# Context stream beside the expert feed-forward: two column tiles of weights in one load, keys and values of two tiles projected in a row, four products of a projection at a step

## The chip, the cores and the metric

One core of one Trainium2 chip runs the whole program as a single launch. The metric is the device time of that launch in microseconds (us); before the change the median of three runs is 2534.96 us (2532.47 to 2540.46). Engines are named as in the profile: PE is TensorE (PEld its weight loads), DVE VectorE, ACT ScalarE, POOL GpSimd, SP SyncE. SP does no arithmetic here; it issues nearly all DMA loads, one after the other.

## What is computed

The reference runs two blocks one after the other. The first mixes tokens and then applies an expert-choice feed-forward with 16 experts; the second works on the output of the first (the "latent" tokens, `x` below) and on a separate context sequence of 256 tokens. Cut to what matters:

```python
def reference(x, ...):
    x = first_block(x, ...)             # token mixer, then 16 experts of 1024 -> 2816 -> 1024
    return second_block(x, ctx_2, ...)  # context and latents through w_in_2, then 32 small experts

def _expert_choice_ffn(h, ...):
    xs = u[idx]                         # 34 rows for each expert
    hid = silu(xs @ w_gate) * (xs @ w_up)
    y = (hid @ w_down) * g              # scattered back by idx

def mixing_sublayer(u_lat, u_ctx, ...):
    a_ctx, b_ctx, _ = split(u_ctx @ w_in)       # independent of the first block
    _, state_a = run_a(a_ctx, zeros_a)          # gated delta rule, 4 heads, two directions
    _, state_b = run_b(b_ctx, zeros_b)          # RWKV, 8 heads, two directions
    oa_lat, _ = run_a(a_lat, state_a)           # the latents start from the context's states
    ob_lat, _ = run_b(b_lat, state_b)
```

The context's part (projections of `u_ctx` and the two final states) does not depend on the first block, so the kernel can do it at any time before the latents are mixed.

## The kernel before

The program has three stages. `head` does the first block's token mixer. `ffn` does the 16 experts. `lat` does the second block: the latents' mixing, the merge and the second expert layer.

**The experts.** `expert` (L881 to L927) takes an expert in three chunks of hidden columns (1024, 1024 and 768 of 2816). For a chunk it loads `w_gate` and `w_up` (four loads each, of 1024 KB or 768 KB) and `w_down` (four loads, or three in the last chunk, of 1024 KB). The rows of an expert fill only 64 columns of the PE array, so products come in pairs: two products, of 64 columns each, run side by side (the loop over `h` at L890 for the tile `gu`, over `dc` at L908 for the tile `dn`). An expert has 70 such pairs and 35 loads. In the profile an f32 product counts as two instructions, so a pair is four. Between `gu` and `dn` stand the activation (`hid`, L896 to L898) and its transposes (`hb` L902, `hT`). The loads of all experts go through a ring of ten buffers of 1 MB; SP waits at each load for PE to be done with the buffer's last content.

**The context stream.** `ctx_pre` (L930) is a Python generator that issues the context's work in small steps. From expert 1 on, `paced` (L869) counts pairs, and after a pair it lets the stream take as many steps as are due: `CTX_STEPS * pairs // CTX_PAIRS`, with 470 steps spread over 1000 of the 1050 pairs (L62). The stream's instructions are issued after that pair (`beside`, L207). So on PE the stream's products stand between pairs of the experts. A scheduler then orders each engine's queue, and may move an instruction that isn't ready in its own reckoning a few places.

**The projections.** The stream has 18 projections of 128 columns of `w_in_2`: eight for the delta rule (`gdn_in` L1243: keys and values, two head pairs, two tiles each) and ten for RWKV (`mixed` L1418: two of low rank, then key and value for each of four column tiles `j`). `projc` (L1076) is one projection: eight products with the transposed context `cuT` (128x256 each, the full array of 128 columns) into one bank `pc`; it yields after each product, so a projection is eight steps. `rwkv_prep` (L1493) projects key and value of its own tile `j` and then goes on with the scaling and the recurrences of that tile.

**Its loads.** `ahead_loader` (L256) has four buffers of 512 KB and keeps three loads ahead of the projection that reads; a load is 128 columns, so a row of it in memory is 512 bytes. These loads stand on SP in between the experts' loads (the DMA issue itself is L252, in `loader`).

Of the kernel before, what the change touches and what calls it, by code (L numbers as in the profile page):

```python
# [10 lines left out]
F32 = mybir.dt.float32  # L11
# [5 lines left out]
P = 128  # L17
D = 1024
KD = D // P
# [39 lines left out]
LBANKS = dict(pa=2, pc=2, pd=1, pb=2, pe=1)  # L59
LPARTS = (3, 5)  # L60

CTX_STEPS, CTX_PAIRS = 470, 1000  # L62

PCOL, PCOL_N = _layout([
    ("mix_norm_g", 8), ("conv_w", 40), ("conv_b", 8), ("ret_gn_g", 4), ("mlstm_gn_g", 4),
# [97 lines left out]
class Net:  # L163
# [89 lines left out]
            return lambda k, cs=slice(None): t[:, k, cs]  # L253
        return load

    def ahead_loader(self, bufs, cols):  # L256

        get, todo, there = self.loader(bufs), iter(cols), []
        ahead = len(bufs) - 1

        def load(c):
            while len(there) < ahead + 1:
                n = next(todo, None)
                if n is None:
                    break
                there.append((n, get(n)))
            n, w = there.pop(0)
            assert n == c
            return w
        return load  # L270

    def rload(self, src):
# [657 lines left out]
    def ctx_pre(self):  # L930

        tc, nc, I = self.tc, self.nc, self.I
        self.SA = [self.S.tile([P, 4, P], F32, name=f"SA{d}") for d in range(2)]
        self.SB = [self.S.tile([P, 4, 64], F32, name=f"SB{d}") for d in range(2)]
        for s in self.SA + self.SB:
            nc.gpsimd.memset(s, 0.0)
        with tc.tile_pool(name="CW", bufs=2, reuse_waits="tile") as CW, tc.tile_pool(name="C", bufs=1, reuse_waits="tile") as C:
            bufs = [CW.tile([P, SLOTW], F32, name="w") for _ in range(2)]
            cols = [gi * 512 + hp * 256 + j * P for hp in range(2) for gi in (1, 2) for j in range(2)]
            cols += [2064 + ci * P for ci in [12, 13] + [4 * gi + j for j in range(4) for gi in (1, 2)]]  # L940
            load = self.ahead_loader([b[:, i * D:(i + 1) * D] for b in bufs for i in range(2)], cols)
            with tc.tile_pool(name="C0", bufs=1, reuse_waits="tile") as T:

                rw = T.tile([P, KD, 36], F32, name="crw")
                self.router_load(rw)
                src = T.tile([P, 2, D], F32, name="csrc")
                nc.gpsimd.dma_start(src, I["ctx_2"][0].rearrange("(t p) d -> p t d", p=P))
                yield
                b = self.bank("ebs")[:, :36]
                for k in range(KD):  # L950
                    nc.tensor.matmul(b, self.mcol[:, 0, 24 + k:25 + k].to_broadcast([P, P]), rw[:, k, :], start=(k == 0), stop=(k == KD - 1))
                    yield
                ob, _ = PROW["router_grp_b_2"]
                self.lbias = self.pers.tile([P, 36], F32, name="lbias")
                nc.vector.tensor_add(self.lbias, b, self.prow[:, ob:ob + 36])
                xn = T.tile([P, 2, D], F32, name="cxn")
                self.norm256(T, src, xn, "css")
                gs, sh = self.mod_cols(T, "norm_mix_g_2", 1, 0, 1, "cmc")
                yield
                uT = yield from self.affT(C, xn, gs, sh, "cuT")  # L960
            with tc.tile_pool(name="CG", bufs=1, reuse_waits="tile") as G:
                gates = yield from self.gdn_gates(G, uT)
                for hp in range(2):
                    qkv = []
                    yield from self.gdn_in(G, uT, False, hp, load, qkv)
                    x = yield from self.gdn_products(G, qkv, False)
                    for d in range(2):
                        yield from self.gdn_dir(G, d, False, 2 * hp, gates, x, self.SA, False, None)
            with tc.tile_pool(name="CR", bufs=1, reuse_waits="tile") as R:
                yield from self.rwkv(R, R, uT, self.SB, False, load, ("pb", "pb", "pb"))  # L970
# [102 lines left out]
            yield  # L1073
        return uT

    def projc(self, w, uT):  # L1076

        b = self.bank("pc")[:, :256]
        for k in range(KD):
            self.nc.tensor.matmul(b, w(k), uT[:, k, :], start=(k == 0), stop=(k == KD - 1))  # L1080
            yield
        return b

    def advance(self, queue, n):
# [158 lines left out]
    def gdn_in(self, W, uT, lat, hp, load, qkv):  # L1243
# [5 lines left out]
        for gi in range(0 if lat else 1, 3):  # L1249
            dst = W.tile([P, 2, 256], F32, name=f"gx{gi}", tag="giB" if gi == 2 and not lat else f"gx{gi}",  # L1250
                         bufs=2 if lat and gi < 2 else 1)
            for j in range(2):
                pj = yield from self.projc(load(gi * 512 + hp * 256 + j * P), uT)
                raw = W.tile([P, 256], F32, name="graw", bufs=1)
                nc.scalar.copy(raw, pj)
                c = 4 * gi + h0 + j
                cw = lambda k: self.pc("gdn_conv_2", c * 5 + k)
                tmp = W.tile([P, 256], F32, name="gcv", bufs=2)
                nc.vector.tensor_scalar(tmp, raw, cw(2), None, op0=ALU.mult)
                for k in (0, 1, 3, 4):  # L1260
                    s = k - 2
                    a, e = max(0, -s), 256 - max(0, s)
                    nc.vector.scalar_tensor_tensor(tmp[:, a:e], raw[:, a + s:e + s], cw(k), tmp[:, a:e],
                                                   op0=ALU.mult, op1=ALU.add)
                self.sigmoid(dst[:, j, :], tmp)
                nc.gpsimd.tensor_mul(dst[:, j, :], dst[:, j, :], tmp)
            if gi < 2:
                for j in range(2):
                    sq = W.tile([P, 256], F32, name="gsq", tag="gcv", bufs=2)
                    nc.scalar.activation(sq, dst[:, j], AF.Square)  # L1270
                    b = self.bank("gn")[:, :256]
                    nc.tensor.matmul(b, self.ct("ones"), sq, start=True, stop=True)
                    nc.scalar.activation(sq, b, AF.Ln, bias=self.eps)
                    nc.scalar.activation(sq, sq, AF.Exp, scale=-0.5)
                    nc.vector.scalar_tensor_tensor(dst[:, j], dst[:, j], 1.0 if gi else P ** -0.5, sq, op0=ALU.mult,
                                                   op1=ALU.mult)
                    if not lat:
                        yield
            qkv.append(dst)
# [112 lines left out]
    def rwkv(self, W, F, uT, S, lat, load, tags, start=None):  # L1392
# [24 lines left out]

        def mixed(ci, dst):  # L1418

            pj = yield from self.projc(load(B0 + ci * P), uT)  # L1420
            pad = F.tile([P, 258], F32, name="rpd", bufs=1)
            nc.gpsimd.memset(pad[:, 0:1], 0.0)
            nc.gpsimd.memset(pad[:, 257:258], 0.0)
# [28 lines left out]
        env = dict(W=W, F=F, lat=lat, na=na, T1=T1, Ne=Ne, lo=lo, nwa=nwa, omk=omk, mixed=mixed, S=S, tags=tags)  # L1452

        if not lat:
            for j in range(4):
                x = {}
                yield from self.rwkv_prep(j, env, x)
                for d in range(2):
                    yield from self.rwkv_scale(j, d, x, env)
# [35 lines left out]
    def rwkv_prep(self, j, env, x):  # L1495
# [7 lines left out]
            x["g2"] = W.tile([P, P], F32, name="rg2", bufs=2)  # L1503
            self.dma.dma_start(x["g2"], self.I["rwkv_g2_2"][0][:, j * P:(j + 1) * P])
        for gi, name in ((1, "k"), (2, "v"), (0, "r")):
            if lat or gi:
                x[name] = F.tile([P, 256], F32, name="rx" + name, bufs=1)
                yield from env["mixed"](4 * gi + j, x[name])
        kk = x["kk"] = F.tile([P, 256], F32, name="rkk")
# [744 lines left out]
```

## Time and profile before

| | us |
|---|---|
| median of three runs | 2534.96 |
| lowest and highest | 2532.47, 2540.46 |
| the profiled execution's own time | 2544.69 |
| its span, from the first to the last instruction | 2542.9 |
| experts' stage in it (first `gu` to last `dn`) | 294.9 to 1722.7, 1427.8 long |
| PE busy over the span | 2343.9 (92%) |

The profiled execution is 0.4% above the median of the runs. In the page the DMA engines are at nine tenths or more from a tenth of the span to two thirds of it, while PE is at nine tenths too, so the page alone doesn't tell which of the two sets the pace there; the rows below are read for that. A "busy" PE is only an engine with a matmul in its pipeline.

### The profile page before, as it was taken

Reading aid. Unit: us, or ns where it says so; the run is one execution under the profiler, and the core shown is the slowest. Engines: PE = TensorE matmul, PEld = TensorE weight load, DVE = VectorE, ACT = ScalarE, POOL = GpSimd, SP = SyncE. Lnnn points to the kernel's source line nnn. Section 1 sums busy time; section 2 is a strip of 40 time slices with the busy share of each in tenths; the row PEclk is TensorE's granted clock in tenths of the full one; section 3 lists DMA queues with packets and bytes.
Section 4 is the critical chain, followed back from the end, with each engine's and each line's share of the span. In section 5 each row is a group of like instructions: output and inputs, shape, how many; then the busy total and the mean of one; then the engine's idle time right before and its main releaser. Section 6 shows DMA issues by size and latency. Waiting matters only on the chain. (4 is left out here: it accounts for less than half of the span.)

```text
span 2542.9 us, 45236 instructions
## 1 busy us (share of the span) xinstructions
PE 2343.9 (92%) x18736; PEld 1251.7 (49%) x18736; DVE 994.2 (39%) x2419; ACT 655.4 (26%) x1652; POOL 350.8 (14%) x627
## 2 busy tenths in 40 slices
PE   7997799999989999999999999987988999989997
PEld 6765334334334333333334333336767777865564
DVE  6655311232222213313313313215576473645545
ACT  4443111221111112212112212214444333522221
POOL 3101100010000101101101101103253232300000
PEclk9998899999999999999999999998979788999999
DMA  7664999998999999999999999994301112689995
GB/s 242 228 235 140 332 407 403 400 400 331 401 382 337 394 369 379 396 397 383 374 409 377 389 407 390 377 407 119 93 22 45 44 27 60 227 273 363 367 366 186
DMA packets 328177, 755.07 MB, mean 297 GB/s; under 512 B 13088, under 2 KB 167376, under 8 KB 324896
## 3 DMA queue, kind: packets, MB, share of 16 engines
q1 hardware_dynamic: 326464, 747.67, 79.6%
q0 software_dynamic: 1504, 4.46, 0.6%
q8 instruction: 150, 2.46, 0.4%
q14 instruction: 59, 0.48, 0.1%
HBM read 751.03 MB, written 1.05 MB: 296 GB/s over the span
## 5 line engine op out<-in xcount | busy, mean ns | idle before, releaser
L891 PE MATMUL gu<-w,xs 128*64 128x512 f32 (+1 forms) x3072 | 682.1, 571 | 2.8 <-DMA w<-in_w_up 1.8
L909 PE MATMUL dn<-w,hT 128*64 128x512 f32 x1408 | 336.5, 604 | 19.1 <-ACT hT L317 17.4
L891 PEld LDWEIGHTS gu<-w,xs 128*64 128x64 f32 x3072 | 196.1, 137 | 289.2 <-issue 271.1
L1080 PE MATMUL pc<-luT,w 128*128 128x256 f32 x688 | 180.0, 403 | 0.5 <-ACT early L300 0.3
L909 PEld LDWEIGHTS dn<-w,hT 128*64 128x64 f32 x1408 | 88.7, 137 | 164.9 <-issue 132.1
L1080 PEld LDWEIGHTS pc<-luT,w 128*128 128x128 f32 x688 | 127.9, 197 | 18.6 <-ACT early L300 0.7
L2110 PE MATMUL egu<-w,exs 128*64 128x256 f32 x1024 | 123.2, 383 | 0.0
L897 DVE TENSOR_TENSOR hid<-hid,gu 128x512 f32<-128x512 f32 (+1 forms) x48 | 30.7, 640 | 203.4 <-ACT hid L302 197.4
L1080 PE MATMUL pc<-cuT,w 128*128 128x256 f32 x288 | 99.2, 429 | 0.0
L1080 PEld LDWEIGHTS pc<-cuT,w 128*128 128x128 f32 x288 | 43.3, 188 | 107.8 <-issue 104.3
L2110 PEld LDWEIGHTS egu<-w,exs 128*64 128x64 f32 x1024 | 74.6, 137 | 39.4 <-issue 6.9
L300 ACT ACTIVATE hid<-gu 128x512 f32<-128x512 f32 (+1 forms) x48 | 26.8, 559 | 238.1 <-PE gu L891 238.1
L1643 POOL TENSOR_SCALAR rsw<-rSU,rwc 64x64 f32<-64x64 f32 x112 | 38.2, 341 | 290.8 <-DVE rSU L1659 280.2
L898 DVE TENSOR_TENSOR hid<-hid,gu 128x512 f32<-128x512 f32 (+1 forms) x48 | 30.8, 642 | 113.4 <-PE gu L891 111.8
L1599 PE MATMUL rmt<-rT,rBK 128*128 128x128 f32 (+1 forms) x256 | 55.4, 361 | 20.3 <-DVE rT L1586 13.9
L2137 PE MATMUL edn<-w,ehT 128*64 128x512 f32 x256 | 67.7, 597 | 0.7 <-ACT ehT L317 0.5
L295 PE MATMUL pj<-uTh,wp 128*128 128x272 f32 x320 | 65.3, 298 | 0.0
L285 ACT CAST wp<-w 128x1024 fp32r<-128x1024 f32 (+1 forms) x48 | 55.0, 1186 | 39.4 <-DMA w<-in_w_in 20.5
L286 DVE TENSOR_TENSOR wp<-w,wp 128x1024 fp32r<-128x1024 f32 (+1 forms) x44 | 57.5, 1328 | 13.3 <-ACT wp L285 13.3
L1599 PEld LDWEIGHTS rmt<-rT,rBK 128*128 128x128 f32 x256 | 43.8, 225 | 35.6 <-POOL rBK L1564 16.2
L2153 DVE TENSOR_TENSOR acc<-acc,esc 128x512 f32<-128x512 f32 x64 | 41.0, 682 | 42.5 <-PE esc L2152 42.5
L295 PEld LDWEIGHTS pj<-uTh,wp 128*128 128x128 f32 x320 | 51.9, 193 | 8.2 <-issue 4.8
(675 smaller groups left out, 3512.1 us busy)
## 6 DMA issues: line engine op xcount, KB each, us to landing
w<-in_w_down SPq DMA_DIRECT2D x176, 1024.0 KB, 11.0
w<-in_w_gate SPq DMA_DIRECT2D x128, 1024.0 KB, 10.8
w<-in_w_up SPq DMA_DIRECT2D x128, 1024.0 KB, 12.3
w<-in_w_gate SPq DMA_DIRECT2D x64, 768.0 KB, 10.7
w<-in_w_up SPq DMA_DIRECT2D x64, 768.0 KB, 7.3
w<-in_w_in SPq DMA_DIRECT2D x65, 512.0 KB, 4.6
w<-in_moe_w_gate SPq DMA_DIRECT2D x32, 1024.0 KB, 13.2
w<-in_moe_w_up SPq DMA_DIRECT2D x32, 1024.0 KB, 12.2
```

Of the source, the lines that this page charges most:

```text
L285: self.nc.scalar.copy(hi, src)
L286: (eng or self.nc.vector).tensor_sub(lo, src, hi)
L295: self.nc.tensor.matmul(out, a[x], b[y], start=(i == 0 and x + y == 0), stop=(i == n - 1 and x == 1))
L891: ins = nc.tensor.matmul(b[h * 64:(h + 1) * 64, :w], xs[:, k, :], ws(k, slice(h * w, (h + 1) * w)), start=(k == 0), stop=(k == KD - 1))
L898: nc.vector.tensor_mul(hid, hid, gu[1][:, :w])
L909: ins = nc.tensor.matmul(dn[dc * 64:(dc + 1) * 64], hT[:, j, h * 64:(h + 1) * 64], wd(h * nf + j, slice(dc * 512, (dc + 1) * 512)), start= ...
L1080: self.nc.tensor.matmul(b, w(k), uT[:, k, :], start=(k == 0), stop=(k == KD - 1))
L1599: ins = nc.tensor.matmul(b[:, i], BK[:, c0 + i, h:h + 2, :], T[:, h, c0 + i, :, :], start=True, stop=True)
L1643: nc.gpsimd.tensor_scalar(sw[r], SU[r, h, c, :], wc[r, c:c + 1], 0.0, op0=ALU.mult, op1=ALU.add)
L2110: nc.tensor.matmul(b[64 * i:64 * i + 64, x * 256:x * 256 + 256], xs[:, k, i, :], w[i](k), start=(k == 0), stop=(k == KD - 1))
L2137: nc.tensor.matmul(b[64 * i:64 * i + 64, :], hT[:, j, 64 * i:64 * i + 64], wd[i](j, cs), start=(j == 0), stop=(j == 1))
L2153: nc.vector.tensor_add(h[:, t, cs], h[:, t, cs], b)
```

## The change

A projection yields after every fourth product where it belongs to the context (`every=4`), so it is two steps and not eight; the latents keep one product a step. `CTX_STEPS` falls from 470 to 362, which is the 18 times six steps fewer; they are still spread over 1000 pairs. Loads bring 256 columns, two neighbouring tiles, in one DMA of 1024 KB with rows of 1024 bytes, into two buffers; the first pair is loaded when the stream starts, and every first use of a pair starts the load of the next (`pair_loader`). In the RWKV part the keys of two tiles and the values of two tiles are projected in a row before the first of them goes on (`rxk` and `rxv` have two buffers each); `rwkv_prep` does no projection for the context any more.

```diff
-CTX_STEPS, CTX_PAIRS = 470, 1000
+CTX_STEPS, CTX_PAIRS = 362, 1000
...
-    def ahead_loader(self, bufs, cols):
-
-        get, todo, there = self.loader(bufs), iter(cols), []
-        ahead = len(bufs) - 1
+    def pair_loader(self, pool, cols):
+
+        todo, there = iter(cols), {}
+        src = self.I["w_in_2"][0]
+
+        def begin():
+            c = next(todo, None)
+            if c is not None:
+                t = pool.tile([P, KD, 2 * P], F32, name="w")
+                self.dma.dma_start(t, src[:, c:c + 2 * P].rearrange("(k p) c -> p k c", p=P))
+                there[c], there[c + P] = t[:, :, 0:P], t[:, :, P:2 * P]
 
         def load(c):
...
+            if c in cols:
+                begin()
+            t = there.pop(c)
+            return lambda k, cs=slice(None): t[:, k, cs]
+        begin()
         return load
...
-            cols = [gi * 512 + hp * 256 + j * P for hp in range(2) for gi in (1, 2) for j in range(2)]
-            cols += [2064 + ci * P for ci in [12, 13] + [4 * gi + j for j in range(4) for gi in (1, 2)]]
-            load = self.ahead_loader([b[:, i * D:(i + 1) * D] for b in bufs for i in range(2)], cols)
+            cols = [gi * 512 + hp * 256 for hp in range(2) for gi in (1, 2)]
+            cols += [2064 + ci * P for ci in (12, 4, 8, 6, 10)]
+            load = self.pair_loader(CW, cols)
...
-    def projc(self, w, uT):
+    def projc(self, w, uT, every=1):
 
         b = self.bank("pc")[:, :256]
         for k in range(KD):
             self.nc.tensor.matmul(b, w(k), uT[:, k, :], start=(k == 0), stop=(k == KD - 1))
-            yield
+            if k % every == every - 1:
+                yield
         return b
...
-                pj = yield from self.projc(load(gi * 512 + hp * 256 + j * P), uT)
+                pj = yield from self.projc(load(gi * 512 + hp * 256 + j * P), uT, 1 if lat else 4)
...
         if not lat:
+            xs = [{} for _ in range(4)]
             for j in range(4):
-                x = {}
+                x = xs[j]
+                if j % 2 == 0:
+                    for gi, name in ((1, "k"), (2, "v")):
+                        for i in range(2):
+                            xs[j + i][name] = F.tile([P, 256], F32, name="rx" + name, bufs=2)
+                            yield from mixed(4 * gi + j + i, xs[j + i][name])
                 yield from self.rwkv_prep(j, env, x)
...
-            if lat or gi:
+            if lat:
                 x[name] = F.tile([P, 256], F32, name="rx" + name, bufs=1)
```

On PE, where RWKV's first projections stand between the experts' pairs (`gu`, `dn`), before:

```order
L1080 MATMUL pc<-cuT,w 128x256
L891 MATMUL gu<-w,xs 64x512 x4
L1080 MATMUL pc<-cuT,w 128x256
L891 MATMUL gu<-w,xs 64x512 x4
L1080 MATMUL pc<-cuT,w 128x256
L891 MATMUL gu<-w,xs 64x512 x4
L1080 MATMUL pc<-cuT,w 128x256
L891 MATMUL gu<-w,xs 64x512 x6
L1080 MATMUL pc<-cuT,w 128x256
```

And the same place of the changed kernel (L895 is L891 there, L1083 is L1080):

```order
L895 MATMUL gu<-w,xs 64x512 x4
L1083 MATMUL pc<-cuT,w 128x256 x4
L895 MATMUL gu<-w,xs 64x512 x6
L1083 MATMUL pc<-cuT,w 128x256 x4
L895 MATMUL gu<-w,xs 64x512 x6
L1083 MATMUL pc<-cuT,w 128x256 x4
L895 MATMUL gu<-w,xs 64x512 x4
L1083 MATMUL pc<-cuT,w 128x256 x4
L895 MATMUL gu<-w,xs 64x512 x6
```

Products of a projection now stand four in a row, with two or three pairs of the experts in between. Over the whole stage the context's 144 products stand in 139 places before (138 alone, six once in a row) and in 30 places after (25 of four, four of eight, one of twelve).

On SP, the queue of loads at the same place of the program, the experts' loads with the stream's (`in_w_in`) among them, before:

```order
L241 DMA w<-in_w_up 128x2x768
L252 DMA w<-in_w_in 128x8x128
L241 DMA w<-in_w_up 128x2x768 x3
L279 DMA w<-in_w_down 128x2x1024 x3
L241 DMA w<-in_w_gate 128x2x1024 x2
L252 DMA w<-in_w_in 128x8x128
L241 DMA w<-in_w_gate 128x2x1024 x2
L241 DMA w<-in_w_up 128x2x1024 x4
```

And after, where the three last loads of the stream stand (L265 issues a pair):

```order
L241 DMA w<-in_w_gate 128x2x1024 x3
L265 DMA w<-in_w_in 128x8x256
L241 DMA w<-in_w_gate 128x2x1024
L241 DMA w<-in_w_up 128x2x1024 x4
L265 DMA w<-in_w_in 128x8x256
L283 DMA w<-in_w_down 128x2x1024 x4
L241 DMA w<-in_w_gate 128x2x768 x2
L265 DMA w<-in_w_in 128x8x256
```

Half as many loads of twice the size stand in the queue, five to eight of the experts' loads apart here; before, 14 loads of one tile stand among the experts' loads after expert 0, after, seven of two tiles (the rest is loaded ahead, at 14 loads into expert 0, in both).

## Rows read from the trace of the kernel before

**Rows 1.** The page: DMA engines' busy tenths and rate, 40 slices

```profile
DMA  7664999998999999999999999994301112689995
GB/s 242 228 235 140 332 407 403 400 400 331 401 382 337 394 369 379 396 397 383 374 409 377 389 407 390 377 407 119 93 22 45 44 27 60 227 273 363 367 366 186
```

**Rows 2.** Windows by expert (1, 2, 7, 11, 12, 14, 15): engines' busy us, clock, DMA

```profile
core 0: us, PE busy (x) PEld busy (x) DVE busy (x) ACT busy (x) POOL busy (x), PEclk, DMA share, GB/s
...
362.30:449.40 87.10, 83.51 (x411) 33.51 (x409) 16.80 (x39) 14.21 (x36) 0.93 (x1) 0.98 1.03 404
449.40:543.80 94.40, 89.69 (x468) 31.32 (x470) 25.85 (x56) 20.84 (x46) 6.34 (x8) 1.00 1.04 397
...
928.10:1019.40 91.30, 85.03 (x679) 32.81 (x679) 25.23 (x59) 18.82 (x45) 10.59 (x23) 1.00 1.01 386
...
1290.70:1380.90 90.20, 86.33 (x653) 31.89 (x651) 23.61 (x55) 17.30 (x40) 9.80 (x21) 1.00 1.00 387
1380.90:1468.00 87.10, 81.03 (x699) 33.61 (x697) 27.20 (x69) 17.41 (x45) 12.60 (x28) 1.00 1.01 394
...
1560.60:1650.20 89.60, 84.67 (x841) 34.37 (x841) 26.90 (x67) 17.56 (x45) 11.99 (x25) 0.98 1.00 378
1650.20:1722.70 72.50, 64.59 (x339) 22.09 (x339) 10.96 (x24) 8.42 (x18) 2.95 (x10) 1.00 1.03 399
```

**Rows 3.** The same view, the whole stage of the experts in one window

```profile
294.90:1722.70 1427.80, 1338.10 (x9522) 516.81 (x9522) 360.70 (x854) 252.16 (x593) 131.72 (x268) 0.99 1.00 386
```

**Rows 4.** Waits of the queue of loads (SP), 440 to 1700: us, times, longest

```profile
engine line waited for: us in total, times, longest us
SPq L241 <- PE gu L891: 396.2, 208, 8.4
SPq L241 <- PE dn L909: 205.7, 58, 9.0
...
SPq L252 <- PE pc L1080: 9.0, 14, 1.8
```

**Rows 5.** Waits of PE, 440 to 1700: us in total, times, longest

```profile
PE hb L902 <- DVE hid L898: 20.4, 31, 1.8
PE dn L909 <- ACT hT L317: 14.9, 25, 0.8
PE rmt L1599 <- DVE rT L1586: 13.9, 6, 3.1
```

**Rows 6.** Timeline of PE, a projection between pairs: start us, us, instructions

```profile
903.42 1.51 PE L891 MATMUL gu<-w,xs 128*64 128x384 f32 x8
904.86 0.70 PE L1080 MATMUL pc<-cuT,w 128*128 128x256 f32 x2
905.49 2.16 PE L891 MATMUL gu<-w,xs 128*64 128x384 f32 x12
907.58 0.70 PE L1080 MATMUL pc<-cuT,w 128*128 128x256 f32 x2
```

**Rows 7.** Timeline of PE in the latents' stage, eight products in a row

```profile
1913.00 3.72 PE L1080 MATMUL pc<-luT,w 128*128 128x256 f32 x16
```

**Rows 8.** Timeline of PE, steps of a recurrence between pairs

```profile
1402.12 1.94 PE L909 MATMUL dn<-w,hT 128*64 128x512 f32 x8 [0.69 <-ACT hT L317]
1403.98 0.33 PE L1647 MATMUL rp<-rP,rY 64*64 64x64 f32 x4
1404.25 1.94 PE L909 MATMUL dn<-w,hT 128*64 128x512 f32 x8
...
1414.80 4.51 PE L891 MATMUL gu<-w,xs 128*64 128x512 f32 x20
```

**Rows 9.** Windows of 25 us; in the second a load of the stream lands

```profile
600.00:625.00 25.00, 24.79 (x326) 9.94 (x324) 5.70 (x16) 2.73 (x7) 0.91 (x2) 0.92 0.68 230
...
925.00:950.00 25.00, 24.50 (x102) 7.64 (x98) 5.24 (x9) 3.83 (x7) 0.74 (x3) 1.00 1.04 400
1250.00:1275.00 25.00, 24.21 (x250) 10.37 (x250) 5.93 (x14) 1.91 (x5) 0.46 (x1) 1.00 0.88 322
...
1450.00:1475.00 25.00, 23.61 (x209) 10.34 (x209) 8.38 (x18) 4.81 (x13) 1.26 (x4) 1.00 1.03 410
```

**Rows 10.** The page's DMA issues: count, KB each, median us to landing

```profile
w<-in_w_gate SPq DMA_DIRECT2D x128, 1024.0 KB, 10.8
w<-in_w_up SPq DMA_DIRECT2D x128, 1024.0 KB, 12.3
```

**Rows 11.** Waits of the queue of loads over the whole span

```profile
SPq L252 <- PE pc L1080: 175.2, 39, 20.9
```

**Rows 12.** Waits of PE in the latents' stage, 1900 to 2230

```profile
PE rp L1632 <- DVE rSU L1659: 6.3, 4, 3.0
```

More of the change, by code (lines that the diff above doesn't have):

```diff
@@ L254, in loader @@
         return load
-    def ahead_loader(self, bufs, cols):
-        get, todo, there = self.loader(bufs), iter(cols), []
-        ahead = len(bufs) - 1
-        def load(c):
[L262 to L269, printed above, removed]
+    def pair_loader(self, pool, cols):
[7 more added lines that the diff above has]
+                there[c], there[c + P] = t[:, :, 0:P], t[:, :, P:2 * P]
+        def load(c):
+            if c in cols:
[3 more added lines that the diff above has]
+        begin()
         return load
@@ L937, in ctx_pre @@
         with tc.tile_pool(name="CW", bufs=2, reuse_waits="tile") as CW, tc.tile_pool(name="C", bufs=1, reuse_waits="tile") as C:
-            bufs = [CW.tile([P, SLOTW], F32, name="w") for _ in range(2)]
-            cols = [gi * 512 + hp * 256 + j * P for hp in range(2) for gi in (1, 2) for j in range(2)]
-            cols += [2064 + ci * P for ci in [12, 13] + [4 * gi + j for j in range(4) for gi in (1, 2)]]
-            load = self.ahead_loader([b[:, i * D:(i + 1) * D] for b in bufs for i in range(2)], cols)
+            cols = [gi * 512 + hp * 256 for hp in range(2) for gi in (1, 2)]
+            cols += [2064 + ci * P for ci in (12, 4, 8, 6, 10)]
+            load = self.pair_loader(CW, cols)
             with tc.tile_pool(name="C0", bufs=1, reuse_waits="tile") as T:
@@ L1418, in mixed @@
         def mixed(ci, dst):
-            pj = yield from self.projc(load(B0 + ci * P), uT)
+            pj = yield from self.projc(load(B0 + ci * P), uT, 1 if lat else 4)
             pad = F.tile([P, 258], F32, name="rpd", bufs=1)
```

## The prediction

> **What bounds the kernel now.** Everything the change touches lies in the experts' stage, so I read that stage alone, in this order. First the page's slices [rows 1]: from the sixth to the twenty-seventh the DMA engines are nine tenths busy or more nearly everywhere, at 331 to 409 GB/s. That looks like a stage set by its loads. Then the same stretch by expert [rows 2]: the DMA share stays near 1.0, but the rate moves between 378 and 404 GB/s, so the stream of weights is not always at its top. The top is seen in a window of 25 us without the context's loads [rows 9]: 410 GB/s at a share of 1.03; and 404 over the whole of expert 1 [rows 2]. In between it falls to 322 and even 230 GB/s [rows 9], while PE is busy 24 of 25 us.
>
> Who waits for whom settles it. SP, which issues the loads, waits 396.2 us in 208 waits for `gu` and 205.7 us in 58 for `dn` [rows 4]: the buffers are full, and a load goes out when PE has used one up. In PE's own waits [rows 5] the large ones are the experts' activation (20.4 and 14.9 us) and the stream's recurrences (13.9 us); no load is among them. So PE sets the pace here, with the DMA close behind. How close: the stage moves 386 GB/s x 1427.8 us = 551 MB [rows 3]. At expert 1's 404 GB/s that is 1364 us, 64 us less than the stage takes; at 410 it would be 84 less. PE's time can shrink by some 60 us before the loads bind the stage as a whole, less where they bind a part of it.
>
> **The change, part by part.**
>
> *Four products at a step.* No product is added or removed; what changes is how often the context's products cut into the experts' pairs. The price of one cut is read off the timeline [rows 6]. Eight instructions of `gu` last from 903.42 to 904.86, 1.44 us from start to start; twelve last from 905.49 to 907.58, 2.09 us. Four cost 0.65, so eight would cost 1.30 in an unbroken row, and the cut adds 0.14. The projection's one product (two instructions) holds PE from 904.86 to 905.49, 0.63 us. In a row such instructions come every (3.72 - 0.70)/14 = 0.216 us [rows 6, 7], 0.43 for two; so 0.20 more are the cut's. Together 0.34. With pairs of 512 columns [rows 8]: eight instructions take 1403.98 - 1402.12 = 1.86, in a row 8 x (4.51 - 1.94)/12 = 1.71, so 0.15 there: 0.35 a cut. The order of instructions shows 139 such places before and 30 after, 109 fewer: 109 x 0.35 = **38 us** of PE's time, nothing of it beside other work, since PE is what the stage waits for.
>
> *Fewer steps, spread over the same pairs.* An expert's 70 pairs take 32.9 steps before (470/1000) and 25.3 after. A step that is not a projection adds its matmuls and the cut, about 0.27 + 0.14 = 0.41 us for a small one [rows 8]. So the work moves: between projections an expert becomes lighter, by 7.6 steps or some 3 us; while projections run, heavier, as two steps now bring eight products. By the end of expert 6 the changed order has done 14 of 18 projections, the old one 11. The gain therefore comes late, from expert 7 on.
>
> *What the faster PE runs into.* An expert's weights are 27 loads of 1024 KB and 8 of 768, 34.6 MB, 85.6 us at 404 GB/s. Expert 1 takes 87.1 us at that rate already [rows 2]: its 7.6 fewer steps save next to nothing; I take back 4 us. Experts 11, 12 and 14 take 90.2, 87.1 and 89.6 us and would come down to 83 to 87, at or below 85.6. There the buffers that were full are drawn on; loads are issued ten buffers ahead, some 26 us, and land in 10.8 to 12.3 [rows 10], so some 14 us of work lies ready. Expert 15 has no steps after its first 20 pairs; it takes 72.5 us [rows 2], less than its loads' 85.6, because it lives on that reserve. What the others draw, expert 15 pays. Bounds: 0 (reserve as before) to 13 us (none left); I take 4, nearer to 0, since each run of projections fills it again.
>
> *Waits for the stream's own results.* With more pairs between steps, PE finds results ready more often: two thirds or so of the 13.9 us of `rmt` can go (-9). With a quarter fewer steps to fill the experts' activation gap, its 35.3 us [rows 5] can grow, by a sixth at most (+6), as few steps stood there. I take 0, between the two.
>
> *Loads of a pair.* Seven loads of 1024 KB for 14 of 512 among the experts' loads. The first reader of a pair comes after the last of the one before. One load after the other of the experts costs 2.6 us of the stream; a pair's costs that at least, and no more than two single ones. With a single one in it, a window of 25 us moved 400 GB/s at a share of 1.04, without it 410 [rows 9]: 10 x 25 = 0.25 MB, 0.6 us a load, up to 8 us of DMA for the 14, of which between nothing and all goes. DMA is not what sets the end, so I count 0. SP waits 9.0 us in 14 waits for the old loads' buffers, 1.8 at most [rows 4]; the new ones stand just as far ahead of PE, at the place where their buffer comes free.
>
> The Trainium skill, "DMA: Bandwidth & Descriptors", Specifications, gives 512 bytes as the least transfer for line rate, by which rows of 512 bytes already run at full rate and pairing them brings nothing at all. The trace is slightly against it (400 against 410 GB/s above), and by the rule the sum stays the same, since that term is 0 in it.
>
> *Keys and values of two tiles in a row.* This shifts eight projections and their work on ACT, POOL and DVE; each has two steps, some five pairs, between it and the next. I count 0. *The latents' stage* keeps its instructions, but the scheduler swaps some neighbours in its second half; PE's largest group of waits there is 6.3 us [rows 12]: 0, within 6 either way.
>
> Sum: -38 + 4 + 4 = **-30 us**. The profiled execution (2544.7, span 2542.9) would become 2515; the median of the runs, 0.4% lower, 2535 - 30 = **2505 us**.
>
> **The rivals.**
>
> *The stream of weights takes over.* For it: a share of 1.0 throughout and expert 1 at its top rate. Then experts 7 to 14, 722.1 us now (928.1 to 1650.2) [rows 2], can come down to 8 x 85.6 = 685 and no further (-37); expert 15 starts without a reserve (+13); and the three projections that move into the experts up to 6 bring 3 x 8 x 0.43 = 10 us of products there (+10), which the later ones give back only within that floor. -14, **2521**. Against it: the many full-buffer waits of SP and 64 us of room over the stage.
>
> The Trainium skill, same page and section, puts the limit of HBM for one core at about 358 GB/s, which would make the stream the bound all through. By that limit 551 MB would need 1539 us and nothing could be gained: 2535. The trace excludes it: the stage takes 1427.8 us and reaches 410 GB/s.
>
> *Waits shrink as well.* Wider spacing removes most of `rmt`'s 13.9 us, and the reserve holds in experts 1 and 15 (the two times 4 are not paid): -38 - 9 = -47, **2488**. For it: the longest of those waits, 3.1 us, is about what another pair between two steps gives. Against it: the activation's gap is then less often filled.
>
> *A pair's load holds up the queue: slower.* A pair waits on SP for the last reader of the buffer, and the experts' loads behind it wait too. In the experts' stage such waits reach 1.8 us; elsewhere in this kernel the same wait reached 20.9 [rows 11]. PE feels it once it is longer than the 14 us that lie ready. At 20.9 each of seven would cost 7 us: +49 - 30 = +19, **2554**. It decides from a wait of 14 + 30/7 = 18 us. Against it: the new loads stand in SP's queue some ten loads ahead of PE, as the old ones do.
>
> That the cuts would not become fewer is excluded by the order (30 places).
>
> **How the numbers follow.** The forecast (2495 to 2517) has 0.60, the stream of weights 0.20 (2512 to 2531), shrinking waits 0.10, the held queue 0.04; 0.06 is for shifts in the latents' stage and the activation's gap that eat the gain. A measurement of this kernel tells about 0.3% from no change, that is 7.6 us: faster means below 2527.4, slower above 2542.6. Faster: 0.60 + 0.10 + three quarters of 0.20 = 0.85; same: the other 0.05 and 0.05 of the last case, 0.10; slower 0.05. The range reaches from the shrinking waits to the upper end of the second case: 2487 to 2531, with 0.05 left out below and 0.12 above.
>
> **What would show it.** In the profile after, four products of a projection (eight instructions) should take about 1.9 us and the context's `pc` some 70 us busy (25 x 2.0 + 4 x 3.72 + 5.4, by [rows 7] and 0.216 an instruction) instead of 139 x 0.70 = 97; the stage from first `gu` to last `dn` about 1398 us, with the gain in experts 7 to 14 (83 to 87 us each, 402 GB/s or more) and expert 15 a few us longer. Waits of SP for `gu` and `dn` should fall. If PE's waits for loads appear in experts 7 to 15, the stream has taken over; if `rmt` waits vanish, the third case is there; waits of several us at the pairs' loads on SP with PE waiting for weights would be the fourth. The forecast is wrong at its root if `gu` takes longer in a row than 0.16 us an instruction at 384 columns once the cuts are gone.

## The result: 29 us less, most of it where it was expected

The changed kernel takes 2508.86 us (median of four runs, 2506.38 to 2513.87), the kernel before, beside it on the same chip, 2537.71 (2532.47 to 2546.12): a ratio of 0.9896, 95% interval 0.9875 to 0.9917, or 29 us. A second comparison, on another chip, gives 2512.48 against 2534.69, 0.9908 (0.9879 to 0.9937), 22 us. Forecast were 2505 and 30 us less. The sum came out; the runs below show that several of its terms did not, in opposite directions.

The page of the changed kernel, its DMA rows in 40 slices (they answer to [rows 1]) and the group of the context's projections (busy us, mean ns, idle before):

```profile
DMA  7664999999989999999999999992311103689995
GB/s 238 226 234 133 339 407 402 403 406 396 389 338 391 379 375 405 406 408 405 406 402 387 394 406 408 406 378 68 87 28 46 45 22 86 220 273 363 368 367 184
...
L1083 PE MATMUL pc<-cuT,w 128*128 128x256 f32 x288 | 70.1, 389 | 0.0
```

From the sixteenth slice to the twenty-sixth the rate now lies between 387 and 408 GB/s, mostly at 402 or more, where it swung between 374 and 409 before. The projections are busy for 70.1 us; some 70 were forecast. The windows by expert (experts 1, 2, 3, 7, 11, 12, 14, 15) show where the time went; then the whole stage, and experts 7 to 14 in one window (compare [rows 2, 3]):

```profile
core 0: us, PE busy (x) PEld busy (x) DVE busy (x) ACT busy (x) POOL busy (x), PEclk, DMA share, GB/s
...
361.60:438.40 76.80, 72.53 (x350) 25.27 (x349) 14.41 (x27) 12.02 (x24) 0.94 (x1) 1.00 1.03 404
438.40:540.20 101.80, 99.12 (x741) 48.31 (x741) 31.82 (x78) 25.04 (x63) 8.56 (x11) 1.00 1.03 404
540.20:630.30 90.10, 84.03 (x664) 34.62 (x663) 25.62 (x61) 13.10 (x28) 5.65 (x7) 1.00 1.01 399
...
922.50:1004.50 82.00, 78.17 (x691) 30.92 (x689) 25.15 (x62) 16.18 (x42) 12.19 (x25) 1.00 1.03 406
...
1266.10:1351.70 85.60, 80.74 (x669) 32.11 (x667) 24.90 (x58) 17.42 (x43) 9.76 (x18) 1.00 1.00 388
1351.70:1438.40 86.70, 78.82 (x655) 30.84 (x655) 25.31 (x61) 16.34 (x40) 11.94 (x25) 0.96 1.02 397
...
1523.40:1607.60 84.20, 76.94 (x655) 30.44 (x653) 24.66 (x57) 15.61 (x39) 11.40 (x24) 1.00 1.03 407
1607.60:1689.20 81.60, 67.04 (x332) 20.58 (x331) 10.31 (x22) 8.25 (x17) 2.33 (x8) 1.00 1.02 396
...
295.00:1689.20 1394.20, 1299.61 (x9522) 527.06 (x9522) 363.65 (x854) 252.78 (x593) 132.63 (x268) 1.00 1.01 396
922.50:1607.60 685.10, 635.88 (x5132) 253.64 (x5130) 191.64 (x456) 128.90 (x318) 83.71 (x180) 1.00 1.02 403
```

The stage goes from 1427.8 to 1394.2 us, 33.6 less; about 1398 was forecast. Experts 7 to 14 take 685.1 us instead of 722.1: 37 less, and together just what their loads need at 404 GB/s, though experts 11 and 12 run at 388 and 397. Expert 1 is 10.3 shorter, expert 2 is 7.4 longer, expert 15 is 9.1 longer. What lies behind the stage shows no change: span less the stage's end is 822.9 us after, 820.2 before. A second profile of the changed kernel has 815.7, so a few us can't be read from this.

PE's waits from 440 to 1700 us (us in total, times, longest; compare [rows 5]):

```profile
PE hb L906 <- DVE hid L902: 25.1, 34, 4.1
PE dn L913 <- ACT hT L321: 17.5, 27, 1.0
...
PE rmt L1609 <- DVE rT L1596: 6.1, 4, 2.0
PE gu L895 <- DMA w<-in_w_up: 6.0, 11, 0.6
...
PE gu L895 <- DMA w<-in_w_gate: 3.7, 7, 0.6
```

The recurrences' wait for this result is less than half of its 13.9 us (8.5 with `rmt`'s waits for other engines), the two of the experts' activation have grown by 7.3 together, and a wait is there that was not among the rows of before: PE waits for weights, 11.1 us in the whole stage with those of `dn` (before: 3.1). Nearly all of it stands in expert 15, as the waits of 1607.6 to 1689.2 show:

```profile
PE gu L895 <- DMA w<-in_w_up: 4.4, 8, 0.6
PE gu L895 <- DMA w<-in_w_gate: 3.7, 7, 0.6
...
PE dn L913 <- DMA w<-in_w_down: 1.4, 2, 0.7
```

The queue of loads, in contrast, waits less for PE (440 to 1700, compare [rows 4]); L265 is the issue of a pair's load:

```profile
SPq L241 <- PE gu L895: 287.2, 174, 6.8
SPq L241 <- PE dn L913: 184.3, 61, 11.7
...
SPq L265 <- PE pc L1083: 17.7, 7, 4.6
```

396.2 us of waits for `gu` have become 287.2: buffers are less often full. And the piece of PE's timeline on which the price of a cut can be read again (start, us, instructions):

```profile
640.96 1.99 PE L1083 MATMUL pc<-cuT,w 128*128 128x256 f32 x8
642.88 2.79 PE L895 MATMUL gu<-w,xs 128*64 128x512 f32 x12
645.61 1.99 PE L1083 MATMUL pc<-cuT,w 128*128 128x256 f32 x8
```

Four products take 642.88 - 640.96 = 1.92 us from start to start; 1.9 was forecast. In a row they would take 8 x 0.216 = 1.73: 0.19 for the cut. The twelve instructions of pairs take 645.61 - 642.88 = 2.73, in a row 12 x 0.214 = 2.57 [rows 8]: 0.16. Together 0.35 again.

The pairs' side is not the same for every kind of cut. Further on in the same trace small products of a recurrence (`rp`) stand between the pairs:

```profile
1019.00 2.75 PE L895 MATMUL gu<-w,xs 128*64 128x512 f32 x12
1021.68 0.33 PE L1657 MATMUL rp<-rP,rY 64*64 64x64 f32 x4
1021.94 2.80 PE L895 MATMUL gu<-w,xs 128*64 128x512 f32 x12
1024.56 0.28 PE L1664 MATMUL rp<-rSU,rKt 128*64 128x64 f32 x4
```

Before a product of form 64*64 the twelve take 1021.68 - 1019.00 = 2.68 us, 0.11 more than in a row; before one of 128*64, the pairs' own form, 1024.56 - 1021.94 = 2.62, only 0.05 more.

### The profile page after: what moved, and what is told of

Its sections match the earlier page's. It is cut to its first block, busy times and chain, and to the rows that moved or that the text cites. A ratio compares the mean times of both kernels' runs of the same rounds, so it can differ in the third digit from the quotient of the medians.

```text
span 2512.1 us, 45204 instructions
## 1 busy us (share of the span) xinstructions
PE 2306.6 (92%) x18736; PEld 1261.9 (50%) x18736; DVE 991.3 (39%) x2419; ACT 656.1 (26%) x1652; POOL 352.6 (14%) x627
## 5 line engine op out<-in xcount | busy, mean ns | idle before, releaser
L895 PE MATMUL gu<-w,xs 128*64 128x512 f32 (+1 forms) x3072 | 666.6, 564 | 10.3 <-DMA w<-in_w_up 6.0
L895 PEld LDWEIGHTS gu<-w,xs 128*64 128x64 f32 x3072 | 199.3, 136 | 307.3 <-issue 265.5
L1083 PE MATMUL pc<-luT,w 128*128 128x256 f32 x688 | 178.6, 400 | 1.9 <-DMA w<-in_w_in 1.9
L1083 PEld LDWEIGHTS pc<-luT,w 128*128 128x128 f32 x688 | 126.8, 195 | 19.2 <-DMA w<-in_w_in 2.0
L1083 PE MATMUL pc<-cuT,w 128*128 128x256 f32 x288 | 70.1, 389 | 0.0
L1083 PEld LDWEIGHTS pc<-cuT,w 128*128 128x128 f32 x288 | 52.3, 190 | 27.6 <-issue 20.2
L290 DVE TENSOR_TENSOR wp<-w,wp 128x1024 fp32r<-128x1024 f32 (+1 forms) x44 | 57.5, 1330 | 16.5 <-ACT wp L289 16.4
L1661 DVE COPY rSU<-rp 64x64 f32<-64x64 f32 x64 | 13.7, 215 | 121.9 <-PE rp L1657 120.7
L906 PE MATMUL hb<-ctab,hid 128*128 128x128 f32 x176 | 30.4, 293 | 29.7 <-DVE hid L902 29.5
```

The lines of the kernel that those rows point to most:

```text
L290: (eng or self.nc.vector).tensor_sub(lo, src, hi)
L895: ins = nc.tensor.matmul(b[h * 64:(h + 1) * 64, :w], xs[:, k, :], ws(k, slice(h * w, (h + 1) * w)), start=(k == 0), stop=(k == KD - 1))
```

## The experiments

Theory **cuts**: each cut of the projections into the pairs costs PE time, and PE sets the pace. Rival **loads**: the larger loads help the stream of weights. Rival **stream**: after the change the stream of weights sets the pace in a part of the experts, so that PE's saving is not all realised. The kernel before lies between 2533.0 and 2541.7 us in the four comparisons, so runs of different comparisons are set side by side by their ratio to it; for the changed kernel that is 0.9902, the mean of its two, or 25 us less. Each ratio is open by 0.002 to 0.0035 either way, 4 to 9 us, and the difference of two ratios by more.

### One part at a time

`cuts_alone` is the kernel before with this edit, and the same at the call for the delta rule:

```diff
-CTX_STEPS, CTX_PAIRS = 470, 1000
+CTX_STEPS, CTX_PAIRS = 362, 1000
-            pj = yield from self.projc(load(B0 + ci * P), uT)
+            pj = yield from self.projc(load(B0 + ci * P), uT, 1 if lat else 4)
```

> The kernel before with one part of the change alone: the context's projections bring four products at a step, and 362 steps are spread over the 1000 pairs. The loads of 512 KB and the old order of keys and values stay. Theory 'cuts' (each of some 109 cuts that vanish gives back 0.35 us of PE's time): about the whole gain, 25 to 33 us below the kernel before, near 2509 us, pc some 70 us busy. Theory 'loads' (a good part of the gain comes from the seven larger loads, which leave the stream of weights more room): 10 us or less below the kernel before, 2528 us or more. If the larger loads cost something that the cuts had to pay for, this run is faster than the changed kernel, by up to the 8 us that were the loads' bound.

`loads_alone` is the changed kernel with `every` at 1 and `CTX_STEPS` at 470.

> The changed kernel with one product a step again and 470 steps: of the change only the loads of two tiles and the keys and values in a row are left. Theory 'cuts': no change against the kernel before, within 5 us (2533 to 2543), SP's waits for gu and dn as long as before. Theory 'loads': 10 to 20 us below the kernel before (2518 to 2528). If holding the queue or the new order of keys and values costs time that the cuts' gain covers, it is above 2543.

Measured: cuts alone 0.9915 (0.9888 to 0.9942), 2512.97 against 2533.04, 21 us by the ratio (15 to 28); loads alone 0.9977 (0.9961 to 0.9994), 2529.87, 6 us by the ratio (1.5 to 9.9), 3 by the medians. Together 27: within these intervals the two add up to the whole. The cuts carry four fifths of it, though fewer than the 25 to 33 us expected of them alone, and the theory of the loads as the cause falls. What the loads bring is above nothing; the interval takes in the bound of 5. In expert 1 it is not a faster stream: `loads_alone` runs at 404 GB/s there in 87.0 us, as before [rows 2]. Counted in the traces, where the count comes out a few higher than in the order of the program used below, PE's pairs are interrupted at 10 places fewer (465 against 475), and PE is idle for 84.0 us of the stage instead of 89.7. Whether the pairs' loads or the order of keys and values does it was not separated.

### More and fewer cuts

`every2` and `every8` are the changed kernel with two products at a step (398 steps) and with all eight (344):

```diff
-            pj = yield from self.projc(load(B0 + ci * P), uT, 1 if lat else 4)
+            pj = yield from self.projc(load(B0 + ci * P), uT, 1 if lat else 8)
```

> The changed kernel with two products at a step and 398 steps: 36 more cuts than the changed kernel, some 73 fewer than the kernel before. Theory 'a price by the cut, and room': 36 x 0.35 = 12.6 us above the changed kernel, near 2521. Theory 'the last part of the gain was no longer realised, because the stream of weights binds': less than that, 4 to 8 us above the changed kernel (2513 to 2517), as the first cuts that go are worth their whole price and the last ones less.

> The changed kernel with a tile's whole projection, eight products, at one step, and 344 steps: 18 fewer cuts. Theory 'PE still sets the pace': 18 x 0.35 = 6 us below the changed kernel, near 2502.5 us. Theory 'the stream of weights now binds experts 7 to 10 and 13 to 15': nothing to 2 us gained, 2507 to 2509, with the experts that stand at 406 GB/s unchanged; and a row of products twice as long can draw the reserve of landed weights deeper in the experts up to 6, which would show as longer waits of gu for DMA.

Measured: `every2` 0.9939 (0.9914 to 0.9964), 9 us above the changed kernel by the ratios; `every8` 0.9882 (0.9849 to 0.9916), 5 us below. Each lies between its two expectations, and the intervals take in both: as times these runs don't decide. Their rows do for one stretch. `every8`, experts 7 to 9 (PE's clock, DMA share, GB/s at the end), and PE's waits for weights from 915 to 1270:

```profile
915.90:1167.60 251.70, 231.09 (x1893) 88.83 (x1893) 71.89 (x178) 48.11 (x119) 34.41 (x71) 1.00 1.03 406
```

```profile
PE gu L895 <- DMA w<-in_w_up: 4.6, 9, 0.6
...
PE gu L895 <- DMA w<-in_w_gate: 3.1, 8, 0.6
```

The changed kernel takes 251.6 us for the same three experts (922.5 to 1174.1), before it was 273.5. PE has 2.4 us less to do in `every8` and waits for weights 7.7 us up to expert 10 instead of 1.6, of which 4.3 us instead of none lie in experts 7 to 9: the stretch stays at 406 GB/s and gains nothing. Here the stream is the bound.

### A lighter and a heavier stream

`light_before` and `light_after` leave a tenth of the weights unloaded in the kernel before and the changed one:

```diff
-                ws = self.wload(src[0, e, :, f0:f0 + 2 * w], 2 * w)
+                if c < 2 or src is I["w_gate"]:
+                    ws = self.wload(src[0, e, :, f0:f0 + 2 * w], 2 * w)
```

> The kernel before, with one tenth of an expert's weights not loaded: for the last 384 hidden columns of an expert the four tiles of w_up are left out and the gate's tile is multiplied in their place (part of the computation is changed, PE's instructions are the same). 31.5 instead of 34.6 MB an expert: 78 us at 404 GB/s instead of 85.6. Theory 'PE set the pace before': nearly nothing to gain, as only experts 1 and 15 stand at the stream's rate, 0 to 6 us below the kernel before. If the stream of weights already bound it in several experts, 15 us or more below.

> The changed kernel with the same loads left out. Theory 'the stream has taken over in experts 7 to 10 and 13 to 15': 10 us or more below the changed kernel, so 38 us or more below the kernel before (2495 or less), with the waits of gu and dn for DMA gone, experts 7 to 10 and 13 and 14 at 80 to 84 us and expert 15 near 72. Theory 'PE still sets the pace all through': not more gained than the same edit gains on the kernel before, 0 to 6 us (2500 to 2507).

Measured: 0.9837 (0.9806 to 0.9869) and 0.9663 (0.9635 to 0.9691), 41 us and 86 us below the kernel before. Both are far below what was expected, and the reason is a flaw of the experiment: the scheduler reckons with the loads, and the order of PE's instructions changed with them. The pairs are interrupted at 356 places instead of 471, and at 285 instead of 391. So a part of either gain is again cuts, and the two runs don't show what lighter loads are worth. What remains is a comparison between them: the same edit brought 19 us more on the changed kernel, (0.9902 - 0.9663) - (1 - 0.9837) = 0.0076, though it took away no more places there (106 against 115). The difference stands in PE's idle time: over the stage that falls from 89.7 to 73.1 us in the kernel before and from 94.6 to 59.4 in the changed one, 18.6 us more, and no wait for weights is left in `light_after`. That agrees with the stream as a bound of the changed kernel, but with the order changed as well it is argued and not shown.

`heavy_before` and `heavy_after` were meant to load the stream in experts 7 to 14:

```diff
+                if 7 <= e < 15 and c < 2:
+                    pad = W.tile([P, 512], F32, name="pad", bufs=1)
+                    nc.gpsimd.dma_start(pad, src[0, e, c * P:(c + 1) * P, :512])
```

> The kernel before with four more loads of 256 KB in each of the experts 7 to 14 (1 MB an expert, 8.4 MB in all, into a tile that nothing reads, issued from POOL); PE has the same instructions, interrupted at 473 places (before: 471). At 404 GB/s the eight MB are 20.8 us of the stream. Theory 'PE set the pace before': experts 7 to 14 took 722 us where their loads need 685, so there is room for 37 us: 0 to 5 us above the kernel before. Theory 'the stream was close to binding it, expert by expert': 10 us or more.

> The changed kernel with the same loads added (397 places, 391 without them: some 1 to 2 us of PE). Theory 'the stream has taken over in experts 7 to 14': they stand at their floor of 685 us and go to 706, so 18 to 23 us above the changed kernel. Theory 'PE still sets the pace': 0 to 7 us above it, as on the kernel before.

Measured: 1.0005 (0.9988 to 1.0021) and 0.9934 (0.9910 to 0.9958), the latter 5 us above the changed kernel on the same chip (2517.05 against 2512.48). The experiment missed its place: nothing ties POOL to the expert, so it issued the loads from 271 us on, the last at 979, and nearly all of them lie before expert 7. Experts 1 and 2 and experts 7 to 14 of `heavy_after`:

```profile
361.30:445.20 83.90, 73.70 (x351) 25.23 (x349) 14.40 (x27) 12.00 (x24) 2.51 (x4) 1.00 1.03 403
445.20:557.10 111.90, 104.87 (x743) 48.90 (x741) 32.46 (x78) 25.05 (x63) 11.29 (x16) 0.95 1.00 387
940.20:1625.70 685.50, 635.61 (x5098) 252.87 (x5098) 191.33 (x456) 128.68 (x317) 84.51 (x182) 1.00 1.02 404
```

8.4 MB more, 20.8 us of the stream, cost the kernel before nothing (3 us less to 5 more by the interval) and the changed one some 5 us. So before there was room in the stream up to expert 6, where the loads went. Where the changed kernel pays is not shown: experts 1 and 2 are 17 us longer together in this profile (83.9 and 111.9 us against 76.8 and 101.8), more than the whole difference, expert 2 at a mean clock of 0.95, and expert 1 of `heavy_before` is 7.2 us longer too (94.3), without a cost in the end. Experts 7 to 14, which got almost nothing extra, stand at 685.5 as without it.

### The same program again

> The changed kernel once more, for the comparison on one chip with the three others and for what a second profile of the same program differs by: both theories expect 0.987 to 0.992 of the kernel before; the experts' stage within some 3 us of 1394.2 us if a profile's stage time is good to that, and the 14 us that the loads of pairs alone took off the stage are then real.

Measured: 0.9908, as above. Its stage is 8 us longer than in the first profile, so a profile's stage time is not good to 3 us. Expert 3, experts 7 to 14, the whole stage and expert 15 of the second profile, the granted clock third from the end:

```profile
543.30:635.00 91.70, 85.65 (x662) 34.96 (x663) 25.61 (x61) 13.09 (x28) 5.64 (x7) 0.98 1.00 383
...
930.10:1618.70 688.60, 638.56 (x5132) 253.95 (x5130) 191.65 (x456) 128.85 (x318) 83.67 (x180) 0.99 1.02 403
295.30:1697.40 1402.10, 1308.82 (x9522) 529.36 (x9522) 363.50 (x854) 252.73 (x593) 132.54 (x268) 0.99 1.01 393
1618.70:1697.40 78.70, 66.23 (x331) 20.94 (x331) 10.30 (x22) 8.25 (x17) 2.34 (x8) 1.00 1.02 396
```

Where an expert's mean clock reads 0.98 instead of 1.00, it takes 1.6 us more for the same instructions (90.1 and 91.7 here): for a short part of it the lower level, 1.2 GHz, was granted. Over the 16 experts the missing share of the clock, times the length, is 6.5 us in the first profile, 17.5 in the second and 15.7 in the profile of before. So the 33.6 us between the first profiles flatter the change; with like clocks, the profile of before against this one, it is 25.7: PE is busy for 29.3 us less (1338.1 to 1308.8) and idle for 3.6 more. And the 13.7 us by which the stage of `loads_alone` is shorter than that of before are not all its own: by the times it is 6.

### The same cuts, spread evenly

In the changed kernel two steps bring eight products, so that products come in bursts. `even_pace` lets the context rest for as many steps as it took products at once, and spreads 470 steps again; `even_1040` spreads them over 1040 pairs, `even8` takes eight products at once:

```diff
-CTX_STEPS, CTX_PAIRS = 362, 1000
+CTX_STEPS, CTX_PAIRS = 470, 1000
             if k % every == every - 1:
-                yield
+                for _ in range(every):
+                    yield
```

> The changed kernel, but a projection's four products stand for four steps, after which the context rests for three; 470 steps over 1000 pairs, so that products and other steps are spread as evenly as before. The pairs are interrupted at 371 places (changed kernel 391, before 471), projections stand at 34 (30, 139). Theory 'a price by the place' (0.15 us on the pairs' side, 0.20 on the projection's): 20 x 0.15 - 4 x 0.20 = 2 us below the changed kernel. Theory 'the uneven spread costs': experts 2, 4 and 6, which carry more products in the changed kernel and run at 100 to 102 us with the stream at 353 to 404 GB/s, come down, experts 7 to 10 carry more again and are bound by PE: 6 to 15 us below the changed kernel, near 2495.

> The evenly spread kernel with its 470 steps over 1040 pairs instead of 1000: some 18 steps go into expert 15, which waits 9.5 us for loads in the changed kernel; 392 places instead of 371. Theory 'expert 15 pays for the lost reserve, and PE has idle time there': what leaves experts 0 to 14 is hidden in 15, 3 to 8 us below the evenly spread kernel. Theory 'a price by the place, wherever it is': 21 x 0.15 + 3 x 0.20 = 4 us above it.

> The evenly spread kernel with eight products at a place and eight steps' rest after them: pairs interrupted at 353 places instead of 371, projections at 18 instead of 34. Theory 'PE sets the pace, a price by the place': 18 x 0.15 + 16 x 0.20 = 6 us below the evenly spread kernel, 18 below the changed one. Theory 'the stream binds': experts 8, 9, 11 and 13 stood at 406 or 407 GB/s in the evenly spread kernel already, nothing to 3 us below it.

Measured: `even_pace` 0.9848 (0.9816 to 0.9880), 39 us below the kernel before and 14 below the changed one by the ratios; `even_1040` 0.9837 (0.9804 to 0.9870), no different; `even8` 0.9861 (0.9829 to 0.9893), no different either. `even_pace` and the changed kernel ran on different chips. On the chip on which both ran, the changed kernel took 2511.9 to 2514.9 us and `even8` 2496.1 to 2503.4; by the prices of a place `even8`'s fewer cuts are worth about 8 of the 11 us between the medians. Expert 15, expert 1 and the whole stage of `even_pace`; expert 15 and what lies ahead of it in `even_1040`:

```profile
1609.00:1679.10 70.10, 63.74 (x341) 22.34 (x339) 10.96 (x24) 8.42 (x18) 2.95 (x10) 1.00 1.04 401
361.20:447.50 86.30, 82.74 (x409) 33.79 (x409) 18.58 (x42) 15.50 (x39) 1.66 (x2) 0.98 1.03 404
293.50:1679.10 1385.60, 1301.26 (x9522) 534.29 (x9522) 360.96 (x854) 251.55 (x593) 132.17 (x268) 0.99 1.02 398
```

```profile
1596.90:1682.00 85.10, 76.24 (x649) 29.78 (x647) 24.00 (x59) 15.11 (x40) 11.05 (x25) 0.98 1.01 384
294.10:1596.90 1302.80, 1227.49 (x8875) 502.59 (x8875) 338.81 (x795) 238.49 (x553) 120.54 (x243) 0.99 1.02 399
```

With clocks like those of the second profile above, the stage is 16.5 us shorter at almost the same number of projections' places (34 against 30) and 20 fewer of all. By the prices of a place these are worth 20 x 0.145 - 4 x 0.20 = 2 us; the rest goes with the spread. PE is idle for 84.3 us instead of 93.3, nearly all of it waits for weights that are gone, and busy for 7.5 less, of which 5 are not explained. Two things come back together in this edit, the rest after four products and the old pace of the other steps (32.9 steps an expert, not 25.3); which of them matters was not separated. Expert 1 is back at 86.3 us, PE's waits for weights in the stage fall to 1.5 us (0.8 for `gu`, 0.7 for `dn`) and expert 15 takes 70.1. In `even_1040` the steps moved into expert 15 save 12.7 us ahead of it and cost 15.0 in it: there is no idle time left there to hide them. `even8` has 18 places fewer than `even_pace` and the same stage (1385.8 us): its projections are 3.2 us shorter on PE, its idle time 5.5 us longer.

## Why the prediction held, step by step

- **What bounds the kernel.** Right: PE, with the stream close behind. `cuts_alone` gains 21 us without touching a load, and `heavy_before` takes 20.8 us of added loads at no cost. SP's waits, which the prediction took to settle it, don't tell by themselves: in experts 7 to 9 of `every8`, where the stream is the bound, SP (L241) still waits 46.8 us for `gu` and 18.9 for `dn`; in the same experts before it was 82.0 and 32.2. That PE hardly waited for weights before, 3.1 us in the stage, is the better sign.
- **109 cuts at 0.35 us, 38 us.** The price holds, the count was right for one half of it only. From start to start the projections fall from 89.6 us to 67.9 in both profiles: 21.7, which is 109 x 0.20. The pairs' side, 0.14 to 0.15 us, is paid where pairs are interrupted at all, and such places fell by 80 (471 to 391), not 109, because places that a projection had shared with another step remain: 80 x 0.145 = 11.6. By this count 33 us instead of 38. Measured without PE's idle time, `gu` and `dn` together are 13 us shorter in the first profile and 5 in the second, whose clock is like that of before: PE's part of the gain is 27 to 35 us, and the 33 are an estimate from the prices.
- **Waits, taken as 0.** Right in sum and in kind: `rmt`'s wait for `rT` fell by 7.8 (all of `rmt`'s waits by 5.4), the activation's waits rose by 7.3 from 440 us on. So the rival by which the waits shrink did not come about.
- **Expert 1, little to gain.** Wrong as a mechanism: it became 10.3 us shorter. 76.8 us at 404 GB/s bring 31.0 MB, 3.6 less than it uses; the rest must have landed before. The next experts paid: 1 to 6 together take 560.9 us, before 565.8. In sum the term was little off.
- **Expert 15 pays 4 us.** The mechanism was right, the size was not: 9.1 and 6.2 us, inside the bounds of 0 to 13.
- **The stream takes over (a rival).** It did in part. Experts 7 to 14 together sit at the floor that this rival set, 685 us; in experts 7 to 9 eight products at a place gained nothing over four. With the cuts' 33 us, the 6 of the loads and the place of the steps held even, 39 us are to be had by this estimate, and `even_pace` has them (30 to 47 by its interval); the changed kernel has 22 to 29. The 10 to 17 us between would be the price of the uneven spread. That PE waits for weights in the changed kernel (10 to 11 us of the stage) and hardly in `even_pace` (1.5) is shown; that a reserve was drawn in expert 1 and again from expert 7 on is argued from the rates. The forecast counted 8 for this.
- **Loads of a pair and keys and values in a row, 0.** They bring 6 us (1.5 to 9.9), by a way that stays open.
- **The queue held up by a pair's load.** Not seen: the pairs' loads wait 17.7 us in 7 waits, 4.6 at most, far from the 18 at which it would decide.
- **The latents' stage, 0.** Nothing speaks against it, but one profile each can't show it: before and after differ by 3 us there, the two profiles of the changed kernel by 7.

So, by this reckoning, 5 us too many for the cuts and 2 to 9 too few for the stream were offset by 6 that the loads brought unforeseen. Each of these terms is open by several us. That the sum came out to 1 us in one comparison and 8 in the other is in part luck.

## What to carry to other kernels

A side stream between the instructions of a bound engine is paid by the place, on both sides of the cut; count the places of either side separately, since two kinds of work that share a place pay one side once, and read the price for the form of the product that cuts. Once the cuts are gone, a second bound is near: then it matters how evenly the side work is spread. The likely reason, argued here and not shown by itself, is that a light stretch can't run faster than the loads come once the reserve of landed loads is used up. And two profiles of one program should be compared by the granted clock before a few us between stages are explained.

## What the runs showed that was not expected

- The spread: the same work with nearly the same cuts, spread evenly, is 14 us faster than in the changed kernel by the ratios, 2 of it by the count of places.
- A change of the loads alone moved the order of PE's instructions (356 places instead of 471 in `light_before`), and gained 41 us that way and by the loads together. An experiment on one resource has to be read with the order that it produces.
- The price of a place, 0.14 to 0.15 us on the side of the pairs and 0.20 on that of the full-width products, is the same in both kernels. The Trainium skill, "TensorEngine Tiling (Array Packing)", Key Properties, says that a change of the tiling mode drains TensorE; the trace agrees as far as it goes: a cut by a product of another form (128*128) costs 0.35 us for its two changes, 0.15 of it on the pairs' side, where one of the pairs' own form (128*64) costs 0.05. That it is a drain no run here shows.
- The granted clock differs between two runs of one program: with its dips to the lower level, 1.6 us in an expert whose mean clock is 0.98, the second profile's stage is 8 us longer.
